# A decoder step's second FFN: the lone microbatch sums into another SBUF tile, and the paired operands are formed in another order with other homes

## The chip, the core and the metric

One Trainium2 chip, one of its cores. The metric is the device time of one execution in microseconds (us). The kernel before took 2370.7 us (median of 3 runs, 2370.17 to 2378.49).

## The reference, cut to what matters

One layer of a decoder step for 1056 tokens (1024 of a prompt, 32 of a sample group): a half-step SwiGLU, then an SSM and sliding-window attention side by side, then cross-attention into a memory, then a second half-step SwiGLU. The change lies in the second half-step alone:

```python
def swiglu(x, w_gate, w_up, w_down):
    return (jax.nn.silu(x @ w_gate) * (x @ w_up)) @ w_down

h = h + rms_norm(c, p['xa_post_g'])            # c: output of the memory attention
h = h + 0.5 * rms_norm(swiglu(rms_norm(h, p['ffn2_pre_g']), p['ffn2_w_gate'], p['ffn2_w_up'],
                              p['ffn2_w_down']), p['ffn2_post_g'])
```

D_MODEL is 1024, D_FF is 2816, everything is float32.

## The kernel before, in words

The 1056 tokens are three microbatches t = 0, 1, 2 of NT = 352 tokens. Activations lie with the features on the partitions: a microbatch is a tile of 128 x 8 x 352 floats. Each fp32 product is made of three passes of `fp32r` matmuls (PASSES): weight and operand are each split into a rounded half (ACT copies it, L99) and a rest (DVE subtracts, L100).

Four large SBUF tiles K0 to K3 (2816 floats a partition, one buffer each) are handed from stage to stage. Whoever takes such a tile next waits until its last user is done. At the end of the memory attention they hold:

- K3: the residual stream of microbatch 0. Its operand halves are made at once (`prenorm`, L195), it is stored to DRAM (L1356), and nobody needs the tile after that.
- K2 and K0: the residual streams of microbatches 1 and 2. `after_o` stores them and then normalises them in place (L1362); they are the inputs of the paired stage.
- K1: the attention's value table and two small chunk buffers. Through these the residual of each microbatch is loaded, two chunks at a time (L1219, tile K<-h), and added by DVE (L220). The last chunks of microbatch 2 pass through K1 while the second FFN has already begun.

The second half-step has three stages:

1. `ffn_one` works on microbatch 0 alone, in 11 groups of two of the 22 slices of D_FF. A group's `gate_up` is 96 matmuls (L105); the `down` of the group before it is 48 matmuls (L241) into eight PSUM accumulators. Six PSUM banks rotate. In the first group ACT copies the eight accumulators into a K tile (L245); in every later one DVE adds them (L247). That tile, the microbatch's sums, is K(home), with home 1.
2. `pair_operands` takes microbatches 1 and 2 (`ya` in K2, `yb` in K0) and forms the eight operands of a seven-product scheme of the Strassen kind, each split into two halves (L279 on ACT, L280 on DVE). There are 12 slots `xq` for halves; the last operand, t4, goes into K(home), with home 3. `pair_gate_up` then runs 154 products (L330: 11 pairs of slices, gate and up, seven products each) with temporaries in K2.
3. `pair_down` for microbatch 1, then for microbatch 2, with sums in K1 and K2 and residuals loaded into K0 and K3 (`load_x`, L434), and the last norm (`finish2`).

The order of the instructions on each engine is not the program's order: a scheduler sets it when the kernel is built, by priorities and by a timeline of its own. Each engine then works through its list in that order. SP issues the loads in its list's order; two `raw` buffers take the weights before the split and six `w` buffers after it.

In the code as printed, `xn[0]` is the pair of operand halves of microbatch 0, `xn[1]` and `xn[2]` are the tiles K2 and K0, and `hs` holds the hidden values in DRAM.

Of the kernel before, what the change touches and what calls it, by code (L numbers as in the profile page):

```python
# [7 lines left out]
F32R = mybir.dt.float32r  # L8
# [19 lines left out]
def decoder_step(tc, a, o):  # L28
    nc = tc.nc
    v, sc, gp, pe, sy = nc.vector, nc.scalar, nc.gpsimd, nc.tensor, nc.sync  # L30

    def pool(name, side):
        return tc.alloc_tile_pool(name=name, bufs=1, side=side, reuse_waits="tile")
# [16 lines left out]
    def K(i):  # L50
        return kp_.tile([128, 2816], F32, name=f"K{i}", tag=f"K{i}", bufs=1)

    def K8(i):
        return K(i).rearrange("p (k n) -> p k n", n=NT)
# [30 lines left out]
    def scratch(name, shape):  # L85
        return tc.dram_tile(shape, F32, name=name)
# [8 lines left out]
    def loadw(src, raw=None, width=1024):  # L95
        if raw is None:
            raw = stage(src, width=width)
        w = wp.tile([128, 2, 1024], F32R, name="w", tag="w", bufs=6)[:, :, :width]
        sc.activation(w[:, 0], raw, AF.Copy)  # L99
        v.tensor_sub(w[:, 1], raw, w[:, 0].bitcast(F32))  # L100
        return w
# [113 lines left out]
    def postnorm(y, gi, resid, wide=False, last=False):  # L215
        ch = [y[:, k] for k in range(8)]
        rs = rstd_last(ch) if last else (rstd_wide if wide else rstd)(sqsum(ch))
        for k in range(8):
            v.scalar_tensor_tensor(y[:, k], y[:, k], gain(gi, k), rs, op0=ALU.mult, op1=ALU.mult)  # L219
            v.tensor_add(y[:, k], resid(k), y[:, k])  # L220


    def gate_up(x, w, h, j):
        pg, pu = bank(), bank()
        for p, ww in ((pg, w[0]), (pu, w[1])):
            for k in range(8):
                mm3(p[:, :NT], ww, k * 128, x, k, k == 0, k == 7)
        s, u = R("sg", [128, NT], 2), Q()
        v.tensor_mul(s, pg[:, :NT], x[2])  # L229
        sc.activation(s, s, AF.Silu)  # L230
        v.tensor_mul(u, pu[:, :NT], x[2])  # L231
        v.tensor_mul(s, s, u)  # L232
        split(s, h[:, j, 0], h[:, j, 1])

    def down(acc, w, h, first):
        for cs in (range(4), range(4, 8)):
            p = {c: bank() for c in cs}
            for j in range(2):
                for c in cs:
                    for i, (wa, xa) in enumerate(PASSES):  # L240
                        pe.matmul(p[c][:, :NT], w[j][:, wa, c * 128:c * 128 + 128], h[:, j, xa],  # L241
                                  start=j == 0 and i == 0, stop=j == 1 and i == 2)
            for c in cs:
                if first:
                    sc.activation(acc[:, c], p[c][:, :NT], AF.Copy)  # L245
                else:
                    v.tensor_add(acc[:, c], acc[:, c], p[c][:, :NT])  # L247

    def hidden(bufs):
        return R("hid", [128, 2, 2, NT], bufs, F32R)  # L250

    def ffn_one(x, wg, wu, wd, home):
        acc, held = None, None
        for g in range(NH // 2 + 1):
            now = None
            if g < NH // 2:
                ws = [(loadw(wg[2 * g + j]), loadw(wu[2 * g + j])) for j in range(2)]
                now = hidden(2)
                for j in range(2):
                    gate_up(x, ws[j], now, j)  # L260
            if held is not None:
                ds = [loadw(wd[2 * (g - 1) + j]) for j in range(2)]
                acc = K8(home) if acc is None else acc
                down(acc, ds, held, g == 1)
            held = now
        return acc
# [3 lines left out]
    def slot(dtype=F32R):  # L270
        return xp[0].tile([128, 4, NT], dtype, name="xq", tag="xq", bufs=12)

    def pair_operands(ya, yb, home):
        b11, b21, b12, b22 = ya[:, 0:4], ya[:, 4:8], yb[:, 0:4], yb[:, 4:8]
        ops = {}

        def halves_of(name, x, to=None):
            hi, lo = to or (slot(), slot())
            sc.activation(hi, x, AF.Copy)  # L279
            v.tensor_sub(lo, x, hi.bitcast(F32))  # L280
            ops[name] = (hi, lo)

        t3 = slot(F32)
        v.tensor_sub(t3, b22, b12)
        v.tensor_sub(b12, b12, b11)
        halves_of("t3", t3)
        halves_of("b11", b11)
        halves_of("t1", b12)
        halves_of("b22", b22)
        v.tensor_sub(b22, b22, b12)  # L290
        halves_of("t2", b22)
        halves_of("b21", b21)
        v.tensor_sub(b21, b21, b22)
        last = K8(home).bitcast(F32R)
        halves_of("t4", b21, (last[:, 0:4], last[:, 4:8]))
        return ops

    def pair_weights(src, j, raws):
# [54 lines left out]
    def pair_gate_up(x, wg, wu, hs, home):  # L353
        gs = K8(home).rearrange("p (i k) n -> p i k n", i=2)

        def raws(n):
            if n % 2:
                return [R("raw2", [128, 1024], 2) for _ in range(2)]
            return [wp.tile([128, 1024], F32, name="raw", tag="raw", bufs=2) for _ in range(2)]

        for j in range(NH // 2):
            g = gs[:, j % 2]
            h = hidden(2).bitcast(F32).rearrange("p a b n -> p (a b) n")
            pair_products(pair_weights(wg, j, raws(0)), x, lambda p: sc.activation(g[:, 0], p, AF.Silu),  # L364
                          g[:, 1], g[:, 2], g[:, 3])
            sc.activation(g[:, 1:4], g[:, 1:4], AF.Silu)
            pair_products(pair_weights(wu, j, raws(1)), x, lambda p: v.tensor_mul(h[:, 0], g[:, 0], p),
                          h[:, 1], h[:, 2], h[:, 3])
            v.tensor_mul(h[:, 1:4], h[:, 1:4], g[:, 1:4])
            for i in range(2):  # L370
                sc.dma_start(hs[2 * j + i], h[:, 2 * i:2 * i + 2])

    def pair_down(wd, hs, i, y, parts):
        for c0, n in parts:
            p = [bank() if c < 6 else pbank() for c in range(n)]
            for k in range(NH):
                h, x = slot(), R("raw2", [128, 1024], 2)[:, :NT]
                hi, lo = h[:, 0], h[:, 1]
                sy.dma_start(x, hs[k][:, i])
                sc.activation(hi, x, AF.Copy)  # L380
                v.tensor_sub(lo, x, hi.bitcast(F32))
                w = loadw(wd[k][:, c0 * 128:(c0 + n) * 128], width=n * 128)
                for c in range(n):
                    for q, (wa, xa) in enumerate(PASSES):
                        pe.matmul(p[c][:, :NT], w[:, wa, c * 128:c * 128 + 128], (hi, lo)[xa],  # L385
                                  start=k == 0 and q == 0, stop=k == NH - 1 and q == 2)
            for c in range(n):
                if c % 2:
                    v.tensor_copy(y[:, c0 + c], p[c][:, :NT])
                else:  # L390
                    sc.activation(y[:, c0 + c], p[c][:, :NT], AF.Copy)
# [39 lines left out]
    def load_x(i, src, between=None):  # L431
        x = K8(i)
        for k in range(0, 8, 2):
            sy.dma_start(x[:, k:k + 2], src[:, k:k + 2])  # L434
            if between and k == 0:
                between()
        return x
# [312 lines left out]
    xn, ws, ds = {}, [], []  # L750
# [472 lines left out]
    xa, cx, xn = {}, {}, {}  # L1223
# [150 lines left out]
    def by_chunk(t):  # L1374
        def get(k):
            x = total()
            sy.dma_start(x, hd[2][t][:, k])
            return x
        return get

    def finish2(t, y, home=None):
        if home is None:
            res = by_chunk(t)
        else:
            x = load_x(home, hd[2][t])
            res = lambda k: x[:, k]
        postnorm(y, G_FFN2_POST, res, last=t == 2)
        for k in range(0, 8, 2):
            sc.dma_start(o["yT"][t, :, k:k + 2], y[:, k:k + 2])

    hs = [scratch(f"hs{j}", [128, 2, NT]) for j in range(NH)]
    finish2(0, ffn_one(xn[0], a["wg2"], a["wu2"], a["wd2"], 1))
    xp[0].release()
    xp[0] = pool("x3", "left")
    ops = pair_operands(xn[1], xn[2], 3)
    pair_gate_up(ops, a["wg2"], a["wu2"], hs, 2)
    for i, parts in ((0, ((0, 8),)), (1, ((0, 4), (4, 4)))):
        y = K8((1, 2)[i])
        pair_down(a["wd2"], hs, i, y, parts)
        finish2(1 + i, y, (0, 3)[i])  # L1400
    return end()


# [123 lines left out]
```

## Time and profile before

| what | value |
|---|---|
| median of 3 runs | 2370.7 us |
| the profiled execution's own time | 2370.24 us |
| its span, first to last instruction | 2368.5 us |
| PE busy, share of the span | 2280.2 us, 96% |
| PE weight loads busy | 2175.7 us, 92% |
| DVE busy | 1634.7 us, 69% |
| ACT busy | 838.9 us, 35% |
| mean granted TensorE clock | 0.983 of 2.4 GHz |
| HBM traffic | 115 GB/s over the span |

The busy time is an average over stages. `ffn_one` begins at about 1577 us, the paired stage at 1866 us, `pair_down` at 2161 us. The profile names a tile without its number, so K0 to K3 all read K, and an order of instructions names it with the number. PEld is PE's weight load, which overlaps the matmuls. A busy PE is not PE at its peak.

### The profile page before, as it was taken

Reading aid. Unit: us, or ns where it says so; the run is one execution under the profiler, and the core shown is the slowest. Engines: PE = TensorE matmul, PEld = TensorE weight load, DVE = VectorE, ACT = ScalarE, POOL = GpSimd, SP = SyncE. Lnnn points to the kernel's source line nnn. Section 1 sums busy time; section 2 is a strip of 40 time slices with the busy share of each in tenths; the row PEclk is TensorE's granted clock in tenths of the full one; section 3 lists DMA queues with packets and bytes.
Section 4 is the critical chain, followed back from the end, with each engine's and each line's share of the span. In section 5 each row is a group of like instructions: output and inputs, shape, how many; then the busy total and the mean of one; then the engine's idle time right before and its main releaser. Section 6 shows DMA issues by size and latency. Waiting matters only on the chain.

```text
span 2368.5 us, 37443 instructions
## 1 busy us (share of the span) xinstructions
PE 2280.2 (96%) x14425; PEld 2175.7 (92%) x14425; DVE 1634.7 (69%) x4004; ACT 838.9 (35%) x1645; POOL 16.0 (1%) x54
## 2 busy tenths in 40 slices
PE   8999999999999899999799999996999899999997
PEld 8999999999999899788699879996999899999996
DVE  8756656665665878787767745588666987776464
ACT  6321121122112333435644323453333433344443
POOL 0000000000000000000000000000000000000000
PEclk9999999999999999999899999998999999999998
DMA  4222122221212322544135642363444243326663
GB/s 169 70 70 75 54 65 66 77 79 56 80 55 84 111 89 72 190 137 130 33 114 183 223 141 63 113 216 119 144 138 133 84 157 108 113 97 196 185 192 119
DMA packets 112194, 272.39 MB, mean 115 GB/s; under 512 B 13168, under 2 KB 54128, under 8 KB 110576
## 3 DMA queue, kind: packets, MB, share of 16 engines
q1 hardware_dynamic: 78976, 227.81, 30.6%
q10 hardware_dynamic: 33040, 42.20, 5.0%
q8 instruction: 113, 1.85, 0.3%
q14 instruction: 65, 0.53, 0.1%
HBM read 229.87 MB, written 43.20 MB: 115 GB/s over the span
## 4 chain that ended last, share of the span: by engine, by line
PE 84%; DVE 7%; DMA 5%; ACT 2%; issue 1%; ACTq 0%; SPq 0%; DVEq 0%
PE mm L105 40%; PE mm L241 14%; PE mm L330 12%; PE mm L385 3%; DMA raw<-wd 3%; PE px L105 3%; DVE w L100 1%; PE cv L1279 1%; PE cs L1254 1%; PE ac L877 1%; PE px L495 1%; DVE K L219 1%; PE px L385 1%; PE px L1176 1%; ACT w L99 1%
## 5 line engine op out<-in xcount | busy, mean ns | idle before, releaser
L105 PE MATMUL mm<-X,w 128*128 128x352 f32 x6384 | 1062.0, 326 | 12.2 <-ACT X L195 5.9
L105 PEld LDWEIGHTS mm<-X,w 128*128 128x128 f32 x6384 | 1030.1, 189 | 29.8 <-ACT X L195 7.9
L99 ACT ACTIVATE w<-raw 128x1024 fp32r<-128x1024 f32 (+1 forms) x271 | 265.9, 988 | 509.6 <-PE mm L105 211.8
L100 DVE TENSOR_TENSOR w<-raw,w 128x1024 fp32r<-128x1024 f32 (+1 forms) x271 | 307.0, 1137 | 147.1 <-ACT w L99 145.0
L241 PE MATMUL mm<-hid,w 128*128 128x352 f32 x2112 | 359.0, 328 | 33.3 <-ACT K L245 20.2
L241 PEld LDWEIGHTS mm<-hid,w 128*128 128x128 f32 x2112 | 346.2, 190 | 40.7 <-ACT K L245 20.8
L330 PE MATMUL mm<-xq,w 128*128 128x352 f32 x1584 | 257.8, 322 | 0.9 <-ACT K L364 0.9
L330 PEld LDWEIGHTS mm<-xq,w 128*128 128x128 f32 x1584 | 254.1, 188 | 1.3 <-ACT K L364 1.2
L247 DVE TENSOR_TENSOR K<-K,mm 128x352 f32<-128x352 f32 x320 | 158.4, 518 | 54.5 <-PE mm L241 53.5
L514 DVE TENSOR_TENSOR K<-K 128x128 f32<-128x128 f32 (+7 forms) x796 | 171.7, 250 | 11.3 <-DMA sp<-K 3.2
L385 PE MATMUL mm<-xq,w 128*128 128x352 f32 x924 | 159.5, 326 | 6.0 <-ACT w L99 4.4
L385 PEld LDWEIGHTS mm<-xq,w 128*128 128x128 f32 x924 | 148.9, 188 | 12.8 <-ACT w L99 7.9
L310 ACT ACTIVATE w<-raw 128x512 fp32r<-128x512 f32 x154 | 89.7, 625 | 123.5 <-PE mm L330 76.5
L231 DVE TENSOR_TENSOR q<-mm,rs 128x352 f32<-128x352 f32 x88 | 46.0, 523 | 119.2 <-PE mm L105 119.1
L311 DVE TENSOR_TENSOR w<-raw,w 128x512 fp32r<-128x512 f32 x154 | 101.0, 686 | 6.6 <-ACT w L310 4.3
L116 DVE TENSOR_TENSOR tot<-tot,sq 128x352 f32<-128x352 f32 x179 | 93.0, 521 | 10.8 <-ACT sq L114 7.1
L114 ACT ACTIVATE sq<-K 128x352 f32<-128x352 f32 x170 | 82.0, 491 | 45.4 <-DVE tot L116 34.7
L229 DVE TENSOR_TENSOR sg<-mm,rs 128x352 f32<-128x352 f32 x88 | 46.1, 523 | 74.1 <-PE mm L105 73.7
L183 ACT ACTIVATE hid<-sg 128x352 fp32r<-128x352 f32 x88 | 43.6, 497 | 145.8 <-DVE sg L232 113.7
L230 ACT ACTIVATE sg<-sg 128x352 f32<-128x352 f32 x88 | 43.2, 492 | 140.5 <-DVE sg L229 124.7
L195 ACT ACTIVATE X<-K,c_gains 128x352 fp32r<-128x352 f32 x80 | 44.0, 579 | 43.1 <-DVE K L220 41.7
L184 DVE TENSOR_TENSOR hid<-sg,hid 128x352 fp32r<-128x352 f32 x88 | 45.9, 521 | 14.4 <-ACT hid L183 13.9
(326 smaller groups left out, 2168.2 us busy)
## 6 DMA issues: line engine op xcount, KB each, us to landing
raw<-wd SPq DMA_DIRECT2D x66, 512.0 KB
raw<-wu SPq DMA_DIRECT2D x65, 512.0 KB
raw<-wg SPq DMA_DIRECT2D x64, 512.0 KB
sp<-sp SPq DMA_DIRECT2D x16, 848.0 KB
h<-K ACTq DMA_DIRECT2D x9, 1408.0 KB
raw<-hs SPq DMA_DIRECT2D x66, 176.0 KB
raw<-wd SPq DMA_DIRECT2D x44, 256.0 KB
K<-xT SPq DMA_DIRECT2D x24, 352.0 KB
```

Source lines behind the costliest of these rows:

```text
L99: sc.activation(w[:, 0], raw, AF.Copy)
L100: v.tensor_sub(w[:, 1], raw, w[:, 0].bitcast(F32))
L105: pe.matmul(p, w[:, wa, col:col + 128], x[xa][:, k, :n], start=first and i == 0, stop=last and i == 2)
L114: sc.activation(q, c, AF.Square)
L116: eng.tensor_add(tot, tot, q)
L241: pe.matmul(p[c][:, :NT], w[j][:, wa, c * 128:c * 128 + 128], h[:, j, xa], start=j == 0 and i == 0, stop=j == 1 and i == 2)
L247: v.tensor_add(acc[:, c], acc[:, c], p[c][:, :NT])
L310: sc.activation(w[:, 0], x, AF.Copy)
L311: v.tensor_sub(w[:, 1], x, w[:, 0].bitcast(F32))
L330: pe.matmul(p, w[a_][:, wa, k * 128:k * 128 + 128], x[b_][xa][:, k], start=start and k == 0 and i == 0, stop=stop and k == 3 and i == 2, s ...
L385: pe.matmul(p[c][:, :NT], w[:, wa, c * 128:c * 128 + 128], (hi, lo)[xa], start=k == 0 and q == 0, stop=k == NH - 1 and q == 2)
L514: v.tensor_tensor(out, x, y, op)
```

## The change

The sums of microbatch 0 go to K3 in place of K1. Among the paired operands, t4 was formed last, from `b22 - t1`; now t2 = `b22 - t1` is written over b11, its halves go to the K tile (K1 in place of K3), t4 comes next into ordinary slots, and b22's halves are made last, of an untouched b22. The sums of microbatch 1 go to K3 in place of K1, and the residual of microbatch 2 to K1 in place of K3.

```diff
         halves_of("b11", b11)
         halves_of("t1", b12)
+        v.tensor_sub(b11, b22, b12)
+        k = K8(home).bitcast(F32R)
+        halves_of("t2", b11, (k[:, 0:4], k[:, 4:8]))
+        halves_of("b21", b21)
+        v.tensor_sub(b21, b21, b11)
+        halves_of("t4", b21)
         halves_of("b22", b22)
-        v.tensor_sub(b22, b22, b12)
-        halves_of("t2", b22)
-        halves_of("b21", b21)
-        v.tensor_sub(b21, b21, b22)
-        last = K8(home).bitcast(F32R)
-        halves_of("t4", b21, (last[:, 0:4], last[:, 4:8]))
         return ops
...
-    finish2(0, ffn_one(xn[0], a["wg2"], a["wu2"], a["wd2"], 1))
+    finish2(0, ffn_one(xn[0], a["wg2"], a["wu2"], a["wd2"], 3))
     xp[0].release()
     xp[0] = pool("x3", "left")
-    ops = pair_operands(xn[1], xn[2], 3)
+    ops = pair_operands(xn[1], xn[2], 1)
     pair_gate_up(ops, a["wg2"], a["wu2"], hs, 2)
     for i, parts in ((0, ((0, 8),)), (1, ((0, 4), (4, 4)))):
-        y = K8((1, 2)[i])
+        y = K8((3, 2)[i])
         pair_down(a["wd2"], hs, i, y, parts)
-        finish2(1 + i, y, (0, 3)[i])
+        finish2(1 + i, y, i)
```

The scheduler places the instructions anew. Three places are shown; there is no time in them.

ACT, at the first group's `down` of `ffn_one`, before. K1_16191 (now K3_16191) are the sums of microbatch 0, K0_15541 the residual of microbatch 2, whose squares (L114) feed a norm; w and raw are weights.

```order
L99 ACTIVATE w_16273<-raw_16271 128x1024
L114 ACTIVATE sq_15790<-K0_15541 128x352
L183 ACTIVATE hid_16064<-sg_16173 128x352
L114 ACTIVATE tot_15832<-K0_15541 128x352
L114 ACTIVATE sq_15834<-K0_15541 128x352
L114 ACTIVATE sq_15837<-K0_15541 128x352
L114 ACTIVATE sq_15840<-K0_15541 128x352
L114 ACTIVATE sq_15843<-K0_15541 128x352
L114 ACTIVATE sq_15846<-K0_15541 128x352
L114 ACTIVATE sq_15849<-K0_15541 128x352
L1356 DMA h2_2_128<-K0_15541 128x2816
L114 ACTIVATE sq_15852<-K0_15541 128x352
```

There, the first L245 copy stands behind all of these: behind the eight squares of the finished residual and its store. And now:

```order
L99 ACTIVATE w_16273<-raw_16271 128x1024
L245 ACTIVATE K3_16191<-mm_16192 128x352
L245 ACTIVATE K3_16191<-mm_16193 128x352
L245 ACTIVATE K3_16191<-mm_16194 128x352
L245 ACTIVATE K3_16191<-mm_16195 128x352
L114 ACTIVATE sq_15790<-K0_15541 128x352
L245 ACTIVATE K3_16191<-mm_16224 128x352
L245 ACTIVATE K3_16191<-mm_16226 128x352
L245 ACTIVATE K3_16191<-mm_16227 128x352
L183 ACTIVATE hid_16064<-sg_16173 128x352
L99 ACTIVATE w_16395<-raw_16393 128x1024
L245 ACTIVATE K3_16191<-mm_16225 128x352
```

Four copies follow the weight split at once; the squares of the finished residual come many instructions later.

DVE, at the second `down` of `ffn_one`, now. L219 and L220 are the norm and the residual of microbatch 2, L229 to L232 the gating of a later group, L247 the additions into the sums; before, L219 stood right behind L133, with nothing of `ffn_one` between.

```order
L133 SCALAR_TENSOR_TENSOR y_15794<-sq_15797,y_15794 128x352
L184 TENSOR_TENSOR hid_16276<-sg_16327,hid_16276 128x352
L219 SCALAR_TENSOR_TENSOR K0_15541<-K0_15541,c_gains_79,y_15794 128x352 x8
L231 TENSOR_TENSOR q_16386<-mm_16336,rs_15135 128x352
L220 TENSOR_TENSOR K0_15541<-K1_12245,K0_15541 128x352 x2
L100 TENSOR_TENSOR w_16484<-raw_16482,w_16484 128x1024
L247 TENSOR_TENSOR K3_16191<-K3_16191,mm_16403 128x352
L247 TENSOR_TENSOR K3_16191<-K3_16191,mm_16404 128x352
L247 TENSOR_TENSOR K3_16191<-K3_16191,mm_16405 128x352
L247 TENSOR_TENSOR K3_16191<-K3_16191,mm_16406 128x352
L232 TENSOR_TENSOR sg_16385<-sg_16385,q_16386 128x352
L247 TENSOR_TENSOR K3_16191<-K3_16191,mm_16435 128x352
```

The norm's work now stands between the group's own instructions, and ahead of the additions that free PSUM banks.

DVE, where the paired operands are formed, before and now (128x1408 are operands of half a K tile, 128x512 are weights):

```order
L247 TENSOR_TENSOR K1_16191<-K1_16191,mm_18167 128x352
L247 TENSOR_TENSOR K1_16191<-K1_16191,mm_18168 128x352
L311 TENSOR_TENSOR w_18371<-raw_18348,w_18371 128x512
L247 TENSOR_TENSOR K1_16191<-K1_16191,mm_18197 128x352
L290 TENSOR_TENSOR K0_15541<-K0_15541 128x1408
L247 TENSOR_TENSOR K1_16191<-K1_16191,mm_18198 128x352
```

```order
L247 TENSOR_TENSOR K3_16191<-K3_16191,mm_18167 128x352
L289 TENSOR_TENSOR K2_15148<-K0_15541 128x1408
L247 TENSOR_TENSOR K3_16191<-K3_16191,mm_18168 128x352
L311 TENSOR_TENSOR w_18371<-raw_18348,w_18371 128x512
L247 TENSOR_TENSOR K3_16191<-K3_16191,mm_18197 128x352
L247 TENSOR_TENSOR K3_16191<-K3_16191,mm_18198 128x352
```

The subtraction that forms t2 stands two additions earlier (as L289, before L290).

## Rows read from the trace of the kernel before

**Rows 1.** Spans and granted clock of the core.
```profile
core 0: 2368.5 us, clock 0.983
```

**Rows 2.** Waits, 1540 to 1660 us: us in total, times, longest.
```profile
PE mm L241 <- ACT K L245: 20.2, 1, 20.2
```

**Rows 3.** Timeline of PE, 1560 to 1670 us: start, us, line, count, idle before.
```profile
1608.47 5.02 PE L241 MATMUL mm<-hid,w 128*128 128x352 f32 x30
1613.70 1.23 PE L241 MATMUL mm<-hid,w 128*128 128x352 f32 x6 [0.22 <-DVE q L231]
1616.14 0.86 PE L163 MATMUL px<-tot,ones 128*128 128x352 f32 x2 [1.21 <-DVE tot L116]
1637.24 2.13 PE L241 MATMUL mm<-hid,w 128*128 128x352 f32 x6 [20.24 <-ACT K L245]
...
1641.45 15.53 PE L105 MATMUL mm<-X,w 128*128 128x352 f32 x96
```

**Rows 4.** The chain that ended last, 1606 to 1642 us: start, us, what.
```profile
1617.04 0.54 DVE tot L164
...
1623.27 3.06 DVE K L219 x6
...
1626.79 2.30 DMA K<-h
...
1636.74 0.46 ACT K L245
```

**Rows 5.** Busy time of each engine by stretch (PE, PEld, DVE, ACT, POOL, PEclk, DMA, GB/s).
```profile
1616.98:1637.24 20.26, 0.02 (x1) 0.00 (x1) 16.34 (x33) 4.37 (x10) 0.00 (x0) 0.58 0.24 78
1637.24:1641.45 4.21, 4.21 (x14) 3.70 (x15) 0.99 (x3) 2.47 (x7) 0.00 (x0) 0.60 0.70 288
1641.45:1664.69 23.24, 23.24 (x146) 23.13 (x146) 20.85 (x38) 8.27 (x12) 0.00 (x0) 1.00 0.45 135
...
1711.13:1734.27 23.14, 23.14 (x146) 23.14 (x146) 15.00 (x22) 8.14 (x11) 0.00 (x0) 1.00 0.44 137
...
1842.00:1881.20 39.20, 32.67 (x187) 30.93 (x185) 38.76 (x55) 20.90 (x32) 0.00 (x0) 0.96 0.19 59
```

**Rows 6.** Waits of PE, 1842 to 1881.2 us.
```profile
PE mm L241 <- DVE K L247: 5.7, 5, 2.0
PE mm L330 <- ACT K L364: 0.9, 1, 0.9
```

**Rows 7.** Timeline of ACT's queue, 1496 to 1560 us: the store of microbatch 0.
```profile
1539.73 0.35 ACTq L1356 DMA_DIRECT2D h<-K  x1
```

**Rows 8.** Timeline, 1815 to 1910 us: the end of the operands' forming.
```profile
1864.68 1.62 DVE L290 TENSOR_TENSOR K<-K 128x1408 f32<-128x1408 f32 x1
...
1878.94 1.62 DVE L280 TENSOR_TENSOR K<-K,K 128x1408 fp32r<-128x1408 f32 x1
...
1880.69 0.44 ACT L364 ACTIVATE K<-mm 128x352 f32<-128x352 f32 x1
1881.18 5.58 PE L330 MATMUL mm<-xq,w 128*128 128x352 f32 x32 [0.87 <-ACT K L364]
```

**Rows 9.** Timeline of SP, 2120 to 2369 us: the residual of microbatch 2 at `pair_down`.
```profile
2167.80 1.37 SPq L434 DMA_DIRECT2D K<-h  x3
```

**Rows 10.** DMA issues of the whole kernel: what, count, size of one.
```profile
raw<-wg SPq DMA_DIRECT2D x64, 512.0 KB
...
h<-K ACTq DMA_DIRECT2D x9, 1408.0 KB
```

**Rows 11.** Waits, 1641.45 to 1664.69 us.
```profile
ACT w L99 <- DMA raw<-wg: 6.1, 2, 3.8
```

**Rows 12.** The chain that ended last, 1500 to 2369 us: weights at the start of `ffn_one`.
```profile
1576.22 5.12 DMA raw<-wg
1581.42 0.97 ACT w L99
...
1587.46 1.15 DVE w L100
```

## Prediction

> **What bounds the kernel now.** I read the span and the clock first [rows 1], then the waits of PE, then the timeline of PE and the chain of waits around the longest of them, and last the busy time by stretch. PE is the engine that sets the time: in an ordinary group of `ffn_one` it is busy for all of 23.14 us at a granted clock of 1.00, while DVE is busy for 15.00 us of them [rows 5]. So a microsecond is won only where PE stands still, or runs at the lower clock.
>
> The largest single stop near the change is one wait of 20.2 us, of L241 for ACT's L245 [rows 2]. The PE timeline shows its shape: 36 of the first `down`'s 48 matmuls run (six accumulators, six banks), a two-instruction norm sum follows, and then PE waits 20.24 us for a bank [rows 3]. The chain of waits tells why the bank is late. It runs through the norm of microbatch 2 (L164, L219), through loads of its residual chunks into K1 (K<-h, the first of them shown, 2.30 us, three such steps in all) and only then to the first copy L245 [rows 4]. That copy needs no result of this chain. It writes to K1, and K1 still carries the residual chunks. While PE stands, DVE works 16.34 us and ACT 4.37 us, and the granted clock is 0.58, which is near the lower of the two levels (1.2 of 2.4 GHz); in the 4.21 us behind the stop it is 0.60 [rows 5].
>
> **The change part by part.** *Sums in K3.* K3 held microbatch 0, whose store was issued at 1539.73 [rows 7], 68.7 us before the first L241 of `ffn_one` at 1608.47 [rows 3]; its landing isn't shown, but even all the time since then is more than three times the stop. So the copies should find K3 free. In the new order of ACT they stand right behind a weight split, ahead of the squares of microbatch 2. What goes:
>
> - The stop: 20.24 us [rows 3].
> - The slow restart: 4.21 us for 12 matmuls and a second pair of norm sums [rows 5]. In a full-clock group 144 matmuls take 23.14 us, 0.161 each, so 12 take 1.93; the pair I put at 0.75 us, a little under the 0.86 of the first pair [rows 3]. 4.21 - 1.93 - 0.75 = 1.5 us.
> - The first pair of norm sums: it ran alone, behind 1.21 us of idle [rows 3]. The 36th matmul ends at 1613.70 + 1.23 = 1614.93 and the stop begins at 1617.00, so 2.07 us pass where 0.75 would do. In the new order it stands among the next group's matmuls: 1.3 us.
>
> Together 23.0 us.
>
> *What DVE and ACT did in the stop.* It doesn't vanish. 16.34 us of DVE work now has to fit beside the next groups. An ordinary group leaves DVE 23.14 - 15.00 = 8.14 us. The group right behind the stop shows that this room can be used: there DVE was busy for 20.85 us, 5.85 more than usual, and PE did not idle at all [rows 5]. The displaced 16.34 and those 5.85 make 22.2 us, which is 2.7 groups of room, and the new order spreads them over three to four groups. What is late then is a bank: at the second `down` the additions L247 stand behind eight multiplies L219 and two additions L220. By the spacing of these instructions DVE comes to the first L247 about when PE has filled its first four accumulators, and two more banks are still open to PE. From both sides: the loss can be 0, as in the group behind the stop, and by the nearest bad row it is 5.7 us, the stretch at the end of `ffn_one`, where DVE is busy for 38.76 of 39.20 us and PE waits for L247 [rows 5, 6]. The far bound is all of the displaced work, 16.3 us. I take 1.0 us, near the row of the same place, and keep 0 to 8 for the range. ACT's 4.37 us fit into 23.14 - 8.14 = 15 us of room a group [rows 5] and cost nothing; without that room they would cost those 4.37.
>
> *Loads and stores that move.* The residual chunks K<-h now stand on SP between weight loads, and each needs the L220 that frees its buffer; in the new order the L220 stands ahead of the split that frees the next weight buffer, so the chunk load is not what the weights wait for. The store of microbatch 2 moves from the end of the stop into a later group. It is 1408 KB against 512 KB of a weight piece [rows 10]. Before, it ran at a DMA share of 0.70 and 288 GB/s [rows 5], the next weight split waited up to 3.8 us for its piece [rows 11], and PE still didn't idle [rows 5]. I put it at nothing; what hides it is the six buffers of split weights.
>
> That has a rule against it. The Trainium skill (DMA: Bandwidth & Descriptors, section on issuing engines not being separate DMA queues) says that transfers started by different engines run on the same 16 DMA engines and interleave. By it the store takes its time from the weight load beside it; the row of the 3.8 us wait agrees, and what it would make of the sum is the fourth rival.
>
> *The paired operands.* The work is the same: the same subtractions and splits, each 128x1408 one 1.62 us [rows 8]. Only places change. The subtraction for t2 comes two additions earlier, ahead of one L247 that PE needs only for its fourth product, so it costs nothing as long as the three products before it last; at most it adds the one instruction, 1.62 us. The last split L280 used to read K2, and K2's next user, L364, waited for it, which stopped PE for 0.87 us [rows 6, 8]. Now the last split reads K0, so L364 comes earlier. Gain 0 to 0.9; with the 1.62 against it I take a gain of 0.5. That t2 instead of t4 lies in a K tile changes no matmul's shape.
>
> *`pair_down`.* The load of the residual of microbatch 2 used to need t4's tile, and was issued at about 2167 [rows 9]; it now needs t2's, whose last matmul is earlier, and the order puts its four DMAs a few weight loads sooner. By size it is again 1408 KB, and up to six split weights lie ready for PE. I put it at 0; it could cost 2, or gain what it takes away later.
>
> **Sum.** 20.24 + 1.5 + 1.3 = 23.0; minus 1.0, plus 0.5: 22.5 us less. The profiled execution took 2370.24 us, so 2347.7; the median of the runs shown is 0.46 above that execution, which makes 2348.
>
> **The rivals.**
>
> *DVE gives part of it back.* The displaced norm and the additions L247 share one list, and banks come late in two or three `down`s. For it: the end of `ffn_one`, where just that costs 5.7 us [rows 6]. Against it: the group behind the stop, full at 20.85 us without a PE stop. Loss 5.7 in place of 1.0: 2352.4.
>
> *The change doesn't do what it says.* The first copy might have another hold than K1, for instance ACT's own list, or K3 might be taken. Then the stop stays and only the 0.5 is left: 2369.7. Against it: the chain has the residual chunks of K1 in it [rows 4], and the new order of ACT has moved the copies. A small chance.
>
> *Slower: the weights fall into single file.* Place: the groups of `ffn_one` behind the second `down`. If DVE's list is so full that each weight piece waits for the split of the one before it, a piece costs load, copy and subtraction in a row: 5.12 + 0.97 + 1.15 = 7.24 us [rows 12], six pieces 43.4 us a group against PE's 23.14, 20.3 us lost in every such group. It decides once the six split buffers have run empty; two groups of it lose 40.6 us and more than eat the gain: 2347.7 + 40.6 = 2388. For it: that chain is seen at the start of `ffn_one`. Against it: PE does not stop there, and each group gives DVE 8 us of room to catch up.
>
> *The store collides with the weights.* The rule above, as a mechanism here: the 1408 KB go ahead of a 512 KB piece that PE needs next. At 288 GB/s [rows 5] the store takes 1408 / 288 = 4.9 us, and PE waits them out: 2347.7 + 4.9 = 2352.6. Against it: before, the same store cost PE nothing.
>
> **How the numbers follow.** Chances: the forecast 0.74, DVE 0.14, the store 0.05, no effect 0.05, single file 0.02. From the forecast's own bounds, a loss of 0 in place of 1.0 and a gain of 0.9 in place of 0.5 give 2346.3; an error in the restart or the norm sums, which I priced by the matmuls beside them, puts the low end at 2343. The high end takes in DVE and store, and a loss of 8, with a little of the runs' own scatter: 2357. What lies beyond are the two last cases and the tails of the rest. About 0.5% of this kernel's time, 11.9 us, is what a measurement can tell from no change. The first three cases lie 18 us and more below 2370.7, so faster has 0.93, same 0.05, slower 0.02.
>
> **What would show it.** In the profile after, the wait of L241 for L245 is gone or under 2 us, and the PE timeline runs from the first `down` into L105 without a break, with the granted clock at 1.00. DVE is busy for more than 20 us in each of the next two groups. The second L105 group begins some 23 us earlier than before, and that lead is still there at the first L330 and at the end. It would be wrong if the lead is smaller behind the second or third `down` (DVE), if PE waits for L99 or L100 there (weights), or if the lead is lost at `pair_down`.

## The result, and the profile after

The changed kernel takes 2352.4 us (median of 5 runs, 2350.7 to 2358.9), the kernel before, beside it, 2371.3. The ratio is 0.9919 with a 95% interval of 0.9896 to 0.9943: faster by 0.8%. The prediction was 2348 us, range 2343 to 2357. The medians lie 18.8 us apart, where 22.5 was worked out. The median also lies on the times of two rivals (DVE gives part back, 2352.4; the store collides, 2352.6), but that is chance: neither mechanism shows at the size that its time was made of, as the waits below tell.

The profiled execution took 2350.7 us. First its span and clock, which answer to [rows 1], then the busy shares.

```profile
core 0: 2348.9 us, clock 0.986
```
```profile
PE 2281.9 (97%) x14425; PEld 2178.3 (93%) x14425; DVE 1631.5 (69%) x4004; ACT 839.4 (36%) x1645; POOL 15.9 (1%) x54
```

PE is busy for about as long as before (2280.2 us there), so nearly all that went is time in which it stood. The timeline of PE shows where (start, us, line, count, idle before). These rows answer to [rows 3]:

```profile
1610.34 6.97 PE L241 MATMUL mm<-hid,w 128*128 128x352 f32 x42
1617.15 1.60 PE L105 MATMUL mm<-X,w 128*128 128x352 f32 x9
1618.58 1.13 PE L241 MATMUL mm<-hid,w 128*128 128x352 f32 x6
...
1634.06 5.02 PE L241 MATMUL mm<-hid,w 128*128 128x352 f32 x30
1639.42 1.24 PE L241 MATMUL mm<-hid,w 128*128 128x352 f32 x6 [0.35 <-DVE q L231]
1641.85 2.21 PE L241 MATMUL mm<-hid,w 128*128 128x352 f32 x12 [1.20 <-DVE K L247]
1643.91 15.52 PE L105 MATMUL mm<-X,w 128*128 128x352 f32 x96
```

The first `down` (48 matmuls of L241) runs without a stop, its last six among the next group's L105. The stop of 20.24 us for L245 is gone. At the second `down` two small waits are new, 0.35 and 1.20 us, both for DVE.

Why the copies are early now, by the timeline of ACT at the first `down`: the first four start 1.37 us after the split before them, and they wait for PE's matmuls, not for the chunks.

```profile
1610.54 1.06 ACT L99 ACTIVATE w<-raw 128x1024 fp32r<-128x1024 f32 x1 [0.55 <-PE mm L105]
1612.97 1.93 ACT L245 ACTIVATE K<-mm 128x352 f32<-128x352 f32 x4 [1.37 <-PE mm L241]
```

The chunks K<-h themselves are loaded even later than before (six of the eight are shown; [rows 4] has one at 1626.79); they are just not waited for any more. From the timeline of SP:

```profile
1639.83 0.80 SPq L1219 DMA_DIRECT2D K<-h  x2
1645.29 0.79 SPq L1219 DMA_DIRECT2D K<-h  x2
1650.16 0.80 SPq L1219 DMA_DIRECT2D K<-h  x2
```

What became of DVE's 16.34 us in the stop [rows 5] stands in the busy time by stretch, one row from each start of a `down` to the next (PE, PEld, DVE, ACT, POOL, PEclk, DMA, GB/s):

```profile
1610.34:1634.06 23.72, 23.72 (x148) 23.51 (x147) 18.48 (x33) 11.90 (x19) 0.00 (x0) 1.00 0.41 131
1634.06:1659.27 25.21, 23.67 (x146) 23.09 (x146) 24.24 (x47) 11.39 (x18) 0.00 (x0) 1.00 0.59 188
1659.27:1682.99 23.72, 23.72 (x148) 23.51 (x148) 22.52 (x40) 7.87 (x9) 0.00 (x0) 1.00 0.53 154
1682.99:1706.13 23.14, 23.14 (x146) 23.14 (x146) 16.01 (x25) 8.63 (x11) 0.00 (x0) 1.00 0.50 158
```

The clock is 1.00 throughout. DVE does 81.25 us of work in the four groups, against 60.00 in four ordinary ones of 15.00 [rows 5], so the displaced work is spread over them as 21.25 us. DVE is fullest in the second group (24.24 of 25.21), and only there does PE wait; the third is nearly as full (22.52 of 23.72), and there PE does not wait.

At the other end of `ffn_one` the waits of PE, from 1821.8 to 1866 us, answer to [rows 6]:

```profile
PE mm L241 <- DVE K L247: 5.0, 5, 2.0
PE mm L330 <- ACT w L310: 2.4, 1, 2.4
```

L330's wait for L364 (0.9 us) has gone, and a longer one for a weight split, L310, is there.

To see what belongs to the change and what to chance, each kernel was profiled a second time, unaltered. What was expected of these two runs:

> The changed kernel once more, unaltered, beside the next two. Theory (the 1.9 us by which its first down of ffn_one came later than before's is scatter of the stages ahead of it, whose instructions are the same): that down now begins somewhere between 1608 and 1612 us, and from it to the last down it takes 211.5 us again, to within 0.5. Rival (something of the change reaches these stages): it begins again at 1610.3 to 1610.4 while the kernel before repeats at 1608.5. Time 2350 to 2353 us.

> The kernel before once more, unaltered, for the same question. Theory (scatter): its first down of ffn_one begins elsewhere than 1608.5, between 1608 and 1612 us; from there to the last down 233.5 us, from pair_down's first matmul to the end 207.6 us, both to within 1. Rival: again 1608.5. Time 2370 to 2374 us.

The second profile of the changed kernel came with 2352.2 us (4 runs, 2350.8 to 2353.4; ratio 0.9915, 0.9901 to 0.9930), that of the kernel before with one time of 2370.7 us. The first `down` began elsewhere each time, as scatter would have it. The table has the time between the same landmarks, each read from PE's timeline: the first L241 of `ffn_one`, the first L241 of its last `down`, the first L385 of `pair_down`.

| stretch, us | before, two profiles | changed, two profiles | difference of means | worked out |
|---|---|---|---|---|
| start to the first `down` of `ffn_one` | 1608.47, 1609.09 | 1610.34, 1609.33 | +1.1 | 0 |
| to its last `down` | 233.55, 233.86 | 211.49, 211.32 | -22.3 | -22.0 |
| to `pair_down` | 318.84, 319.55 | 320.33, 320.25 | +1.1 | -0.5 |
| to the end | 207.64, 206.40 | 206.74, 208.10 | +0.4 | 0 |
| span | 2368.5, 2368.9 | 2348.9, 2349.0 | -19.8 | -22.5 |

The second row is the change, and it came out as worked out. The first row is most likely scatter: no instruction was moved ahead of this point, and PE, DVE and ACT work through the same instructions in both kernels up to it. In the two profiles of before and the two of the changed kernel it ranges from 1608.47 to 1610.34 and in the seven kernels below from 1609.28 to 1613.58, whichever home the sums have; but the two of before are the lowest of all eleven, so a small part that belongs to the change is not excluded. The fourth is of the size by which two profiles of one kernel differ (1.2 and 1.4). The third is small but holds in both profiles, and the experiments go after it.

### The profile page after: what moved, and what is told of

Same layout as the page of the kernel before. It is cut to its first block, busy times and chain, and to the rows that moved or that the text cites. A ratio compares the mean times of both kernels' runs of the same rounds, so it can differ in the third digit from the quotient of the medians.

```text
span 2348.9 us, 37434 instructions
## 1 busy us (share of the span) xinstructions
PE 2281.9 (97%) x14425; PEld 2178.3 (93%) x14425; DVE 1631.5 (69%) x4004; ACT 839.4 (36%) x1645; POOL 15.9 (1%) x54
## 4 chain that ended last, share of the span: by engine, by line
PE 85%; DVE 7%; DMA 5%; ACT 2%; issue 1%; ACTq 0%; SPq 0%; DVEq 0%
PE mm L105 39%; PE mm L241 14%; PE mm L330 13%; PE mm L385 3%; PE px L105 3%; DMA raw<-wd 2%; DVE w L100 1%; PE cv L1279 1%; PE cs L1254 1%; PE px L1176 1%; DVE K L219 1%; PE ac L877 1%; PE px L495 1%; PE px L385 1%; DMA K<-h 1%
## 5 line engine op out<-in xcount | busy, mean ns | idle before, releaser
L105 PE MATMUL mm<-X,w 128*128 128x352 f32 x6384 | 1060.8, 325 | 12.3 <-ACT X L195 6.5
L105 PEld LDWEIGHTS mm<-X,w 128*128 128x128 f32 x6384 | 1028.3, 189 | 30.2 <-ACT X L195 8.5
L241 PE MATMUL mm<-hid,w 128*128 128x352 f32 x2112 | 358.6, 328 | 12.6 <-DVE K L247 6.2
L241 PEld LDWEIGHTS mm<-hid,w 128*128 128x128 f32 x2112 | 345.6, 189 | 19.7 <-DVE K L247 8.8
L330 PE MATMUL mm<-xq,w 128*128 128x352 f32 x1584 | 263.5, 323 | 0.0
L330 PEld LDWEIGHTS mm<-xq,w 128*128 128x128 f32 x1584 | 255.9, 188 | 0.4 <-ACT w L310 0.4
L247 DVE TENSOR_TENSOR K<-K,mm 128x352 f32<-128x352 f32 x320 | 158.3, 518 | 52.2 <-PE mm L241 51.3
L385 PE MATMUL mm<-xq,w 128*128 128x352 f32 x924 | 159.1, 326 | 4.6 <-ACT w L99 3.4
L385 PEld LDWEIGHTS mm<-xq,w 128*128 128x128 f32 x924 | 148.8, 188 | 10.7 <-ACT w L99 5.9
L310 ACT ACTIVATE w<-raw 128x512 fp32r<-128x512 f32 x154 | 90.0, 625 | 119.1 <-PE mm L330 83.1
L114 ACT ACTIVATE sq<-K 128x352 f32<-128x352 f32 x170 | 81.9, 490 | 42.7 <-DVE tot L116 34.7
L229 DVE TENSOR_TENSOR sg<-mm,rs 128x352 f32<-128x352 f32 x88 | 46.0, 523 | 72.9 <-PE mm L105 72.5
```

Source lines behind the costliest of these rows:

```text
L105: pe.matmul(p, w[:, wa, col:col + 128], x[xa][:, k, :n], start=first and i == 0, stop=last and i == 2)
L114: sc.activation(q, c, AF.Square)
L310: sc.activation(w[:, 0], x, AF.Copy)
L330: pe.matmul(p, w[a_][:, wa, k * 128:k * 128 + 128], x[b_][xa][:, k], start=start and k == 0 and i == 0, stop=stop and k == 3 and i == 2, s ...
```

## The experiments

**One part alone: the homes.** The kernel before, operands in their old order, with the new homes:

```diff
-    finish2(0, ffn_one(xn[0], a["wg2"], a["wu2"], a["wd2"], 1))
+    finish2(0, ffn_one(xn[0], a["wg2"], a["wu2"], a["wd2"], 3))
-    ops = pair_operands(xn[1], xn[2], 3)
+    ops = pair_operands(xn[1], xn[2], 1)
-        y = K8((1, 2)[i])
+        y = K8((3, 2)[i])
-        finish2(1 + i, y, (0, 3)[i])
+        finish2(1 + i, y, i)
```

> Only the homes move (lone sums to K3, t4's halves to K1, the sums of microbatch 1 to K3, the residual of microbatch 2 to K1); the operands keep the order of the kernel before, t4 last. Theory (the home of the lone sums carries the gain; the new operand order costs about 1.5 us): the stop of L241 for L245 is gone, the second L105 group begins about 22.2 us sooner counted from the first down of ffn_one, the 2.4 us wait of L330 for L310 of the changed kernel is gone and the 0.9 us wait for L364 is back; time 2349 us, 1.5 below the changed kernel. Rival (the new operand order carries part of the gain, and its wait comes from the shifted ffn_one): the wait for L310 stays and the time is 2351 or more.

Measured: 2352.7 us (2349.5 to 2354.5), ratio 0.9912 (0.9897 to 0.9927), the changed kernel's own within its interval. The stop is gone. But the theory's second half fell: the waits at the entry of the paired stage (1844 to 1890 us) are

```profile
PE mm L330 <- ACT K L364: 1.2, 1, 1.2
PE mm L330 <- ACT w L310: 1.2, 1, 1.2
```

2.35 us together by the timeline, against the changed kernel's one of 2.38. The old order of the operands does not take that loss away; it shares it out differently. By its two signs, a wait for L310 that stays and a time of 2351 or more, the rival came true. The next run and the second profile of the kernel before speak against both parts of it: the new order carries no gain, and that profile (shown further below) has a wait for L310 too, with `ffn_one` unmoved. From the last `down` to `pair_down` the run with the homes took 318.6 us, 1.7 less than in the changed kernel, but not by these waits; L247 cost 3.8 there in place of 5.0. The first to the last `down` took 213.7 us in place of 211.5 (last section).

**The other part alone: the operands' order**, with all old homes (t2's halves in K3, the sums of microbatch 0 in K1). As a diff against the changed kernel:

```diff
-    finish2(0, ffn_one(xn[0], a["wg2"], a["wu2"], a["wd2"], 3))
+    finish2(0, ffn_one(xn[0], a["wg2"], a["wu2"], a["wd2"], 1))
-    ops = pair_operands(xn[1], xn[2], 1)
+    ops = pair_operands(xn[1], xn[2], 3)
-        y = K8((3, 2)[i])
+        y = K8((1, 2)[i])
-        finish2(1 + i, y, i)
+        finish2(1 + i, y, (0, 3)[i])
```

> Only the operands' order changes (t2 before t4, b22's halves last, t2's halves in K3); all other homes are those before, the lone sums in K1. Theory (the order alone costs a little): the 20.2 us stop stays, L330 waits 2 to 3 us for L310 in place of 0.9 us for L364, time 1.5 us above the kernel before, 2372. Rival (the order is part of the gain): the stop shrinks, or the paired stage from its first L330 to pair_down gets shorter, and the time falls below 2370.

Measured: 2373.0 us, ratio 1.0001 (0.9989 to 1.0013). The waits from 1600 to 1660 us show the stop untouched:

```profile
PE mm L241 <- ACT K L245: 20.2, 1, 20.2
PE px L163 <- DVE tot L116: 1.2, 1, 1.2
```

At the entry of the paired stage L330 waits 1.5 us for L337 and 0.7 for L310. From the last `down` to `pair_down` it is 318.9 us, as in the kernel before (318.8 and 319.6). So the order of the operands alone is worth nothing that can be measured, and neither the 1.5 us of cost expected nor a gain is borne out; the interval reaches about 3 us to either side, so the time alone doesn't exclude such a cost.

**Is it K1 that holds the copies?** Here all homes stay as before, K1 included; only the residual chunks of microbatch 2 go elsewhere, into the two buffers of the norm's sums:

```diff
+    def by_tot(src):
+        def get(k):
+            x = total()
+            sy.dma_start(x, src[:, k])
+            return x
+        return get
...
-        postnorm(y, G_XA_POST, resid(hd[1][t]), True)
+        postnorm(y, G_XA_POST, by_tot(hd[1][t]) if t == 2 else resid(hd[1][t]), True)
```

> The kernel before, homes and operand order untouched (lone sums in K1); only the last residual chunks of microbatch 2 in after_o are loaded into the two norm-sum buffers instead of K1's chunk buffers. Theory (K1 was held by these chunks): the stop of L241 for L245 is gone or under 2 us, the second L105 group begins 21 to 22.5 us sooner from the first down of ffn_one, time 2347 to 2353 us. Rival (the first copy is held by something else, such as its place in ACT's list or the chain through the norm of microbatch 2): a stop of 15 us or more stays and the time is above 2364.

Measured: 2349.7 us (2346.9 to 2353.0), ratio 0.9902 (0.9883 to 0.9920). The only wait of PE from 1600 to 1660 us is now

```profile
PE mm L241 <- DVE K L247: 0.2, 1, 0.2
```

The sums are in K1, the copies do not wait, and the gain is all there. Together with the two runs above this shows the cause from both sides: the stop goes if the sums leave K1, and also if the chunks leave K1. The norm of microbatch 2, on the chain of [rows 4], is still computed there and stops nothing. Before, the copies also stood late in ACT's list, and in this run they stand early; but the list can have cost little, for in the chain of the kernel before the last reads of K1 are

```profile
1634.97 0.98 DVE K L220 x2
```

and the first copy starts at 1636.74 [rows 4], 0.8 us behind their end. From the first to the last `down` this kernel takes 209.9 us, 1.5 less than the changed one, the 1.55 us of waits at its second `down`. From there to `pair_down` it takes 320.6 us, as much as the changed kernel, though its operands and their homes are those of the kernel before.

**The new wait for L310.** The timeline of the changed kernel, all engines, 1850 to 1864 us:

```profile
1853.04 3.15 DVE L280 TENSOR_TENSOR xq<-K,xq 128x1408 fp32r<-128x1408 f32 x2
...
1856.55 0.68 DVE L316 TENSOR_TENSOR raw<-raw,raw 128x512 f32<-128x512 f32 x1
...
1858.99 0.52 DVE L367 TENSOR_TENSOR hid<-K,mm 128x352 f32<-128x352 f32 x1 [1.33 <-PE mm L330]
...
1859.87 0.68 DVE L317 TENSOR_TENSOR raw<-raw,raw 128x512 f32<-128x512 f32 x1
...
1860.59 1.67 ACT L310 ACTIVATE w<-raw 128x512 fp32r<-128x512 f32 x3
...
1861.27 0.59 PE L330 MATMUL mm<-K,w 128*128 128x352 f32 x2 [2.38 <-ACT w L310]
```

Two splits of operands (L280, t4 and b22, 3.15 us) stand on DVE ahead of the weight sums L316 and L317; ACT's split L310 needs L317, and PE's next product, behind 84 matmuls or seven products, needs L310. So the next run makes b22's halves ahead of t4's, earlier in DVE's list:

```diff
         halves_of("b21", b21)
+        halves_of("b22", b22)
         v.tensor_sub(b21, b21, b11)
         halves_of("t4", b21)
-        halves_of("b22", b22)
```

> The changed kernel, with b22's halves made ahead of t4's instead of behind. Theory (the 2.4 us wait of L330 for L310 comes from two 1.62 us splits standing on DVE ahead of the weight sums of the second set): one split now stands there, the wait falls by about 1.6 us to about 0.8, and the last split reads K2 again, so a wait for L364 of up to 0.9 us may come; time 0 to 1.6 us under the changed kernel, 2349 to 2351. Rival (the wait hangs on ACT's list or on the weights' loads): it stays at 2.4 us and the time is that of the changed kernel.

Measured: 2351.1 us (2349.2 to 2352.4), ratio 0.9907 (0.9891 to 0.9924). The waits there:

```profile
PE mm L330 <- ACT w L310: 0.5, 1, 0.5
PE mm L330 <- DVE w L311: 0.2, 1, 0.2
```

Down by about 1.7 us, the size that the theory gave, and 319.3 us to `pair_down` in place of 320.3. In the time of the whole kernel that is too little to be told from scatter. The reason given is not borne out: all seven splits of operands (L280) stand ahead of L317 on DVE in this run too, for b22's, made earlier, still comes before it. What changed is the place of L367. It multiplies by the product that PE has just finished, so whatever stands behind it waits for PE; in the changed kernel L317 does, and DVE is idle for 1.33 us ahead of L367. Here the scheduler put L317 first:

```profile
1857.70 0.72 DVE L317 TENSOR_TENSOR raw<-raw,raw 128x512 f32<-128x512 f32 x1
1858.78 0.52 DVE L367 TENSOR_TENSOR hid<-K,mm 128x352 f32<-128x352 f32 x1 [0.36 <-PE mm L330]
```

A full list can hold L317 back as well: in the second profile of the changed kernel, in the same order, DVE comes to L367 without idling, and PE's wait is 2.44 us.

**DVE's list at the entry.** If it is DVE's full list that makes these waits, any work taken out of it should end them, not only a split. The last norm of microbatch 0, with eight squares and their sums, stands there, and nothing in the kernel waits for its result. This run moves it behind the third pair of slices:

```diff
-    finish2(0, ffn_one(xn[0], a["wg2"], a["wu2"], a["wd2"], 3))
+    y0 = ffn_one(xn[0], a["wg2"], a["wu2"], a["wd2"], 3)
...
-    pair_gate_up(ops, a["wg2"], a["wu2"], hs, 2)
+    pair_gate_up(ops, a["wg2"], a["wu2"], hs, 2, lambda: finish2(0, y0))
...
         for j in range(NH // 2):
+            if j == 3 and mid:
+                mid()
```

> The changed kernel with the last norm of microbatch 0 put behind the third of the eleven pairs of slices of the paired stage, instead of in front of that stage. Theory (the waits at the entry of the paired stage are DVE's full list there: 44 of 45 us busy): with eight additions of the norm out of it (3.4 us of DVE), the wait of L330 for L310 falls from 2.4 to under 1 us, from the last down to pair_down it takes 318 to 319 us in place of 320.3; time 1 to 2.5 us under the changed kernel run beside it. Rival (that wait is set by the two operand splits and the weights alone): 2.4 us and 320.3 us stay.

Measured: 2348.4 us (4 runs, 2346.8 to 2350.7), ratio 0.9903 (0.9886 to 0.9919); the changed kernel beside it on the same chip 2352.2, its lowest run 2350.8. By stretch, from the first L330 to `pair_down`, first the changed kernel, then this one:

```profile
1844.33:2142.16 297.83, 295.45 (x1838) 294.64 (x1837) 236.04 (x409) 123.28 (x207) 0.00 (x0) 1.00 0.37 119
```
```profile
1845.86:2139.81 293.95, 293.95 (x1837) 293.94 (x1837) 235.24 (x407) 123.80 (x209) 0.00 (x0) 1.00 0.36 120
```

PE is busy for all of 293.95 us: no wait is left in the paired stage, though the two splits are where they were. From the last `down` it is 316.9 us, 3.4 less, more than the 1.3 to 2.3 expected. So the rival, the two splits and the weights alone, is out: moving the norm ends the wait. That it does so by relieving a full DVE list is argued, not shown: here, too, L317 stands ahead of the product's user (L369 in this kernel), and DVE even idles just before it.

```profile
1857.78 0.52 DVE L339 TENSOR_TENSOR q<-q,mm 128x352 f32<-128x352 f32 x1 [1.06 <-PE mm L330]
1858.22 0.68 DVE L317 TENSOR_TENSOR raw<-raw,raw 128x512 f32<-128x512 f32 x1
...
1859.77 0.53 DVE L369 TENSOR_TENSOR hid<-K,mm 128x352 f32<-128x352 f32 x1 [0.44 <-PE mm L330]
```

The squares left ACT's list as well. No run changes the order of L317 and L367 alone.

**Both chunk buffers and b22's halves**, on the changed kernel (the edits of two runs above):

> The changed kernel with b22's halves ahead of t4's (as in the run of that edit) and the last residual chunks of microbatch 2 loaded into the norm-sum buffers instead of K1. Theory (what the displaced norm gives back at the second down is 1.5 us of waits, and the other chunk buffers take it away): from the first down to the last down 209.9 us in place of 211.5, waits there under 0.5 us in place of 1.5; the wait for L310 about 0.5; time 2 to 3 us under the changed kernel run beside it, about 2348.5. Rival (the waits at the second down do not hang on the chunks): 211.5 us stays there and the time is 1 us under the changed kernel or the same.

Measured: 2350.0 us (2346.1 to 2352.4), ratio 0.9905 (0.9890 to 0.9920). First to last `down` 210.1 us with one wait of 0.4, and 0.4 and 0.3 us at the entry: both steps as expected. The time is 2.2 below the changed kernel's, with overlapping runs: that is inconclusive. Its first `down` began at 1613.58, the latest of all profiles, so the profiled execution lost ahead of the stage what it won in it.

**All three edits together**, on the changed kernel:

> The three edits of the runs before together on the changed kernel: b22's halves ahead of t4's, the last residual chunks of microbatch 2 in the norm-sum buffers, the last norm of microbatch 0 behind the third pair of slices. Theory (they act in different places and add up): from the first to the last down 210 us in place of 211.5, no wait of L330 over 0.3 us, from the last down to pair_down 317 us in place of 320.3; 4 to 5 us under the changed kernel, about 2347. Rival (the kernel with the late norm alone has it all, since what is left is scatter): 2348 to 2349.

Measured: 2347.9 us (4 runs, 2346.4 to 2350.9), ratio 0.9898 (0.9882 to 0.9915). First to last `down` 210.2 us, no wait of L330, 317.8 us to `pair_down`. It is the lowest median of all and under both kernels; from the late norm alone (2348.4), the rival's case, it can't be told, and the changed kernel was not run beside it.

## Why the prediction was right, and where it missed

*The stop, the restart and the lone norm sum* (23.0 us) **held.** From the first L241 to the group that begins at 1643.91 the changed kernel is 22.65 us faster (1664.69 - 1608.47 = 56.22 against 33.57); with 1.0 given back, 22.0 had been worked out. In the second pair of profiles it is 23.1. The nearness is in part luck, for two errors of 1.0 us cancel. Up to the second `down` it won 24.6 us (48.35 against 23.72); 0.6 of them come back in the third group, where the second norm sum now stands, which leaves 24.0 in place of 23.0. The other error is the next term. That the copies had no other hold was argued from the chain; the run with the chunks elsewhere shows it.

*DVE's give-back* (1.0 us) **held** in its place and was put too low: the waits are 0.35 + 1.20 us at the second `down`, which takes 9.85 us from its start to the next L105 where it took 7.87, so 2.0 us. The chain of waits runs just through the instructions that were named:

```profile
1636.36 2.57 DVE K L219 x5
1638.93 0.43 DVE q L231
1639.37 0.87 DVE K L220 x2
1640.23 1.13 DVE w L100
1641.37 0.44 DVE K L247
...
1641.85 2.21 PE mm L241 x12
```

The rest of DVE's work is hidden: in the third group DVE is busy for 22.52 of 23.72 us, and PE for all of them.

*Loads and stores* (0) **held.** The store of microbatch 2 now goes out at 1655.89, and the longest wait of a weight split for its load from 1652 to 1690 us is 2.4 us; PE doesn't wait there at all. The rule of the Trainium skill that transfers from different engines interleave (DMA: Bandwidth & Descriptors, section on issuing engines not being separate DMA queues) is not contradicted by this, but it cost PE nothing, so the fourth rival is out. Nor does DVE wait for a chunk load ahead of the additions that PE waits for.

*The paired operands* (a gain of 0.5) **failed.** Two things were wrong in it. The wait of 0.87 us for L364, which was to go, was read from one execution as if it belonged to the kernel. The second profile of the kernel before has, in the same place,

```profile
PE mm L330 <- ACT K L364: 1.2, 1, 1.2
PE mm L330 <- ACT w L310: 0.8, 1, 0.8
```

2.0 us together, with not one instruction moved. And what is late next was sought in the operands alone: L364 no longer stops PE, but the weight sum L317 of the second set is late in its place (2.38 us), behind L367 on DVE's list. From the last `down` to `pair_down` the changed kernel took about 1.1 us more by the means of two profiles each. That the step cost them is not shown: the run with the chunks elsewhere has the old operands and takes 320.6 us there, and the two parts alone take 318.6 and 318.9. The order of the operands by itself is worth nothing that can be measured (1.0001).

*`pair_down`* (0) **held** within the scatter: +0.4 us where two profiles of one kernel differ by up to 1.4. The residual of microbatch 2 is issued at 2136.60, before the stage begins (at 2142.16), where its first DMA had been issued at 2166.85, 6 us into it ([rows 9] has the other three), and nothing waits for it.

The spans differ by 19.8 us on average where 22.5 was worked out. Of the 2.7 missing, 1.6 lie between the last `down` and `pair_down` (1.1 lost, 0.5 not won), 0.4 at the end, and 1.1 lie ahead of the change, against 0.3 more gained in `ffn_one`. Why the start of `ffn_one` scatters by some 5 us was not looked into.

## What to carry to other kernels

A tile that is handed from stage to stage holds back its next user until the last small use of any part of it is done, and the profile shows that as a wait for the engine that writes next, not for the tile: walk the chain of waits until something turns up that the waiting instruction doesn't need. Give the next stage a tile whose last use lies well back, or move the late small use to buffers of its own; both gave the same here. Work that a stop had hidden comes back on the other engines, so look for the stretch where their lists are full, and take out of it what nobody waits for. Where an instruction comes late, see too what stands ahead of it in its engine's list: one that itself waits holds it back even where the engine has time to spare.

## What the runs showed that was not expected

Small stops of PE can cost more than themselves. At the second `down` the run with the homes alone waits 1.28 and 1.19 us, and the 12 matmuls behind run at a granted clock of 0.56, near the lower of the two levels (1.2 of 2.4 GHz). By its timeline and by stretch:

```profile
1641.49 1.24 PE L241 MATMUL mm<-hid,w 128*128 128x352 f32 x6 [1.28 <-DVE q L231]
1643.93 3.52 PE L241 MATMUL mm<-hid,w 128*128 128x352 f32 x12 [1.19 <-DVE K L247]
```
```profile
1643.93:1647.28 3.35, 3.35 (x12) 3.35 (x13) 3.35 (x9) 0.26 (x1) 0.00 (x0) 0.56 0.54 177
```

In the changed kernel, with 0.35 and 1.20 us ahead, the same 12 take 2.21 us. The run with the late norm has 0.54 and 1.21 ahead and takes 3.74; the one with b22's halves first has 0.71 and 1.20 and takes 2.21. So 1.3 to 1.5 us hang on whether the clock falls at such a place, and the length of the stops alone doesn't tell; what does is open. One program does both. At the last `down` of the kernel before, behind the same stop (of the four before it only the first differs, 1.44 and 0.73 us), its two profiles read

```profile
1862.49 3.74 PE L241 MATMUL mm<-hid,w 128*128 128x352 f32 x12 [2.00 <-DVE K L247]
```
```profile
1862.71 2.21 PE L241 MATMUL mm<-hid,w 128*128 128x352 f32 x12 [2.00 <-DVE K L247]
```

at a granted clock of 0.52 and of 1.00. That bears on the third row of the table. From the last `down` to the first L330, and in the 40 us behind, the clock is 1.00 and 1.00 in the run with the operands' order alone (318.9 us to `pair_down`), and 0.92 and 0.96 both in the second profile of the changed kernel and in the run with the chunks elsewhere (320.3 and 320.6), though PE waits less there. A difference of one microsecond in this stretch may be no more than that.
